# Attention's transpositions and 64-wide scores on halves of the array's rows, in common sections, with all eight PSUM banks in one ring

## The chip, the core and the metric

The kernel runs on one core of one Trainium2 chip. A core has a matrix engine (TensorE, with an array of 128 rows and 128 columns), VectorE, ScalarE, GpSimd, a queue that issues transfers (SyncE), an on-chip memory of 128 partitions (SBUF), and eight accumulation banks (PSUM) into which TensorE writes. The metric is the device time of one execution in microseconds; lower is better. In the profile PE is TensorE's matmuls, PEld its weight loads, DVE VectorE, ACT ScalarE, POOL GpSimd and SP SyncE.

## What is computed

A trunk of two layers over 512 tokens of width 1024, all in float32. Each layer has three attentions side by side on one projection of the normed input, a gated sum of them, and a feed-forward part with a short convolution. The parts that matter here are the three attentions:

```python
z_na, c_q, c_kv, k_rope, z_gq, z_gkv, z_gate = jnp.split(h @ w_in, offs, axis=-1)
# A, neighbourhood: 8 heads of 64, grid of 8 x 64 tokens, 16 columns around each, bias by position
s = jnp.einsum('bqhd,brqchd->bhqrc', q_r, k_win) * scale + bias
p = jax.nn.softmax(s.reshape(B, H, GRID_W, win_r * NA_WIN_C), axis=-1)
out = jnp.einsum('bhqrc,brqchd->bqhd', p, v_win)
# B, latent: 4 heads, 128 plain values and 64 rotary ones, the rotary key shared by the heads
s = (jnp.einsum('bqhd,bkhd->bhqk', qn, k_nope) + jnp.einsum('bqhr,bkr->bhqk', qp, k_pe)) * scale
o = jnp.einsum('bhqk,bkhd->bqhd', jax.nn.softmax(s, axis=-1), v)
# C, window: 8 heads of 64 on 2 key heads, blocks of 128 with their neighbours, a sink logit per head
s = jnp.einsum('bnqkgd,bnjkd->bnkgqj', qb, kw) * scale
p = jax.nn.softmax(jnp.concatenate([s, sink_b], axis=-1), axis=-1)[..., :-1]
o = jnp.einsum('bnkgqj,bnjkd->bnqkgd', p, vw)
merged = gates[0] * (y_na @ w_br_na) + gates[1] * (y_mla @ w_br_mla) + gates[2] * (y_gqa @ w_br_gqa)
```

## The kernel before

Everything is kept transposed: channels lie on partitions, the 512 tokens along the free dimension. TensorE's operands are of the type fp32r. To keep float32's accuracy each operand is a pair of a high part (rounded to fp32r, by ScalarE) and a low part (the rest, by VectorE); `split` (L147) makes the pair. A product is then three matmuls, high x high, high x low and low x high (`mm3`, L159, its matmuls on L164 to L166). `dense` (L168) is such a product over a weight block that `fetch` (L109) loads from memory and splits ahead of time; a block over 1024 channels is 24 matmuls of 128x128 weights and 512 moving columns.

The order of the work is a list of steps written by hand in `schedule` (L251, the list from L290); `run` calls `do_<step>` for each, and TensorE and the transfer queue keep that order. ScalarE and VectorE are ordered by a scheduler, in which the attention's steps (`ATTN`, L38) have priority. Dense steps (`gate`, `br`, `qn`, `kn`, `naq`, `gq` and so on) stand between the attention's steps.

Each attention has the same stages. Scores are formed by TensorE in a bank (`do_ms` L515 latent, `do_ns` L634 neighbourhood, `do_gs` L781 window). VectorE and ScalarE make the softmax of them in a tile `pt`. TensorE turns 128x128 blocks of `pt` by a transposing matmul, in which the block is loaded as weights and an identity (`idf`) streams through (`do_mt` L536, `do_nt` L666, `do_gt` L823, on L540, L671 and L830). `split` takes the turned blocks out of the bank into a pair `ph`, `pl`, and TensorE multiplies that with the values (`do_mp`, `do_np`, `do_gp`).

Where a score runs over 64 values only, half of the array's rows would be empty. The kernel before fills them: `stack` (L225) puts the high part of a query (or key) on 64 partitions and its low part on the other 64, `swap` (L230) makes a copy with the halves exchanged, and two matmuls over all 128 rows give all four products of high and low parts. They are L523 and L524 (the rotary part of the latent scores, 512 columns), L652 and L653 (neighbourhood, 256 columns), L799 and L800 (window, 384 columns, or 256 at the ends).

The banks are given out by `bank` (L103) from groups that each stage sets with `banks`: in the latent attention two for dense products, three for scores, two for turned blocks and one for the values' product. A step takes the next bank of its group, and waits until that was read. The steps are fine-grained: a latent head's scores come as two halves of two query blocks, its sixteen blocks are turned in two halves of eight, and each half is followed by half of the values' product.

Of the kernel before, what the change touches and what calls it, by code (L numbers as in the profile page):

```python
# [17 lines left out]
P = 128  # L18
L = 2
D = 1024  # L20
S = 512
# [16 lines left out]
ATTN, ATTN_PRIO = ("ms", "mt", "mp", "ns", "nt", "np", "gs", "gt", "gp"), 100  # L38
RAWB, WB, GZB, GPB, PRIO = 3, 3, 5, 3, 300
HALVES = ((slice(0, 64), slice(64, 128)), (slice(64, 128), slice(0, 64)))  # L40
# [18 lines left out]
class Trunk:  # L59
# [153 lines left out]
    def rope(self, pool, ps, rows, ct, st, nb=2):  # L213
        nc = self.nc
        sw = pool.tile([P, S], F32, tag="ph", name="rsw", bufs=nb)
# [3 lines left out]
        t = pool.tile([P, S], F32, tag="pl", name="rot", bufs=nb)  # L219
        self.mul(t[:rows], ps[:rows], ct[:rows])  # L220
        self.mul(sw[:rows], sw[:rows], st[:rows])
        nc.vector.tensor_add(t[:rows], t[:rows], sw[:rows])
        return t

    def stack(self, dst, src, half):  # L225
        a, b = HALVES[half]
        self.nc.scalar.copy(dst[a], src[a])
        self.nc.vector.tensor_sub(dst[b], src[a], r32(dst)[a])

    def swap(self, dst, src):  # L230
        self.nc.scalar.copy(dst[0:64], r32(src)[64:128])
        self.nc.scalar.copy(dst[64:128], r32(src)[0:64])
# [18 lines left out]
    def schedule(self, l):  # L251
# [39 lines left out]
        s += [("kn", 0), gate(), "mla_attn", ("qn", 1), ("kn", 1), ("ms", 0, 0), ("ms", 0, 1), gate()]  # L291
# [4 lines left out]
        s += [gate(), ("mt", 3, 0), ("nak", 0), ("mp", 3, 0), ("mt", 3, 1), ("nav", 0), ("mp", 3, 1)]  # L296
        s += ["na_open", ("nvt", 0), ("ns", 0), ("naq", 1), ("ns", 1), ("nav", 1), ("br", 1, 0), ("nt", 0)]
        s += [("nak", 1), ("np", 0), ("nt", 1), ("br", 1, 1), gate(), ("np", 1)]
        for p in (1, 2):
            h = 2 * p  # L300
            s += [("nvt", p), ("ns", h), ("naq", p + 1), ("ns", h + 1), ("nav", p + 1), ("nt", h)]
            s += [("nak", p + 1), ("np", h), ("nt", h + 1), ("br", 1, p + 1), gate(), ("np", h + 1)]
        s += [("nvt", 3), ("ns", 6), ("br", 1, 4), ("ns", 7), ("br", 1, 5), gate(), ("nt", 6)]
        s += [("br", 1, 6), gate(), ("np", 6), ("nt", 7), ("br", 1, 7), gate(), ("np", 7)]
        s += ["gq_open", "gk", ("gq", 0), "gv", ("gq", 1), "gvt", gate(), ("br", 0, 0), ("br", 0, 1)]
        s += [("gs", 0, 0), ("gq", 2), ("gs", 0, 1), ("gq", 3)]
# [3 lines left out]
        s += [("gt", 7, 0), ("gt", 7, 1), gate(), ("gp", 7), "br012", ("br", 2, 3)]  # L310
# [144 lines left out]
    def do_kr(self):  # L455
# [11 lines left out]
        self.stack(self.kr[0], t, 0)  # L467
        self.swap(self.kr[1], self.kr[0])
# [19 lines left out]
    def do_qr(self):  # L488
        st = self.weights(self.spec())
        self.qr = []  # L490
        for i in range(2):
# [3 lines left out]
            for j in range(2):  # L495
                q = self.mp.tile([P, S], F32R, tag=f"qr{2 * i + j}", name="qr")
                self.stack(q, t, j)
                self.qr.append(q)

    def do_mla_attn(self):  # L500
        self.banks(d=[0, 1], s=[2, 3, 4], tp=[5, 6], po=[7])
# [13 lines left out]
    def do_ms(self, h, half):  # L515
        nc, mm = self.nc, self.nc.tensor.matmul
        for b in (2 * half, 2 * half + 1):
            bs = slice(b * P, (b + 1) * P)
            s = self.bank("s")
            mm(s, self.qn[h][0][:, bs], self.kn[h][0], start=True, stop=False)  # L520
            mm(s, self.qn[h][0][:, bs], self.kn[h][1], start=False, stop=False)
            mm(s, self.qn[h][1][:, bs], self.kn[h][0], start=False, stop=False)
            mm(s, self.qr[h][:, bs], self.kr[0], start=False, stop=False)  # L523
            mm(s, self.qr[h][:, bs], self.kr[1], start=False, stop=True)  # L524
            nm = self.small.tile([P, 2], F32, tag="nm", name="nm", bufs=6)
            pt = self.mp2.tile([P, S], F32, tag="pt", name="pt", bufs=6)
# [9 lines left out]
    def do_mt(self, h, half):  # L536
        for kc in (2 * half, 2 * half + 1):
            tp = self.bank("tp")
            for b in range(4):
                self.nc.tensor.transpose(tp[:, b * P:(b + 1) * P], self.pts[h, b][:, kc * P:(kc + 1) * P], self.idf)  # L540
            self.pp[h, kc] = [self.mp2.tile([P, S], F32R, tag=t, name=t, bufs=2) for t in ("ph", "pl")]
            self.split(*self.pp[h, kc], tp)

    def do_mp(self, h, half):
        if half == 0:
            self.po = self.bank("po")
        kcs = (2 * half, 2 * half + 1)
        hs = slice(h * P, (h + 1) * P)
        self.mm3(self.po, [tuple(v[:, hs] for v in self.V[kc]) for kc in kcs], [self.pp[h, kc] for kc in kcs],
                 half == 0, half == 1)  # L550
        if half == 1:
            self.y[1, h] = self.ypair("ya", h)
            self.split(*self.y[1, h], self.po)

    def do_na_open(self):
        nc = self.nc  # L560
        self.banks(d=[0, 1, 2], s=[3, 4], tp=[5, 6], po=[7])
# [18 lines left out]
    def do_naq(self, p):  # L580
        ps = self.dense(self.spec(), self.h)
        if p == 0:
            self.q1, self.q2, self.k1, self.vt, self.vs, self.nc_ = {}, {}, {}, {}, {}, {}
# [6 lines left out]
    def na_q(self, p):  # L590
        for j in range(2):
            h = 2 * p + j
            self.q1[h] = self.np.tile([P, S], F32R, tag="q1", name="q1", bufs=3)
            self.q2[h] = self.np.tile([P, S], F32R, tag="q2", name="q2", bufs=3)
            self.stack(self.q1[h], self.nc_["q", p], j)
            self.swap(self.q2[h], self.q1[h])
# [9 lines left out]
    def na_k(self, p):  # L606
        for j in range(2):
            k = self.np.tile([P, S + P], F32R, tag="k1", name="k1", bufs=3)
            self.pad(r32(k))
            self.stack(k[:, 64:576], self.nc_["k", p], j)  # L610
            self.k1[2 * p + j] = k
# [22 lines left out]
    def do_ns(self, h):  # L634
        nc, mm = self.nc, self.nc.tensor.matmul
        tm = self.np.tile([P, 3, 256], F32, tag="tm", name="tm")
        nc.vector.tensor_tensor(tm, self.nmask, self.tb[h][:].rearrange("p (o k) -> p o k", o=1).to_broadcast([P, 3, 256]), ALU.add)
        if h + 4 < 8:
            self.na_table(h + 4)
# [467 lines left out]
```

## Time and profile before

| | |
|---|---|
| median of 3 runs | 1702.47 us (1701.95 to 1702.61) |
| profiled execution, from its first to its last instruction | 1700.3 us |
| the median stands above that span by | 2.2 us |
| granted TensorE clock | 1.000 |
| instructions of the profiled execution | 21121 |
| transfers | 155.38 MB, mean 91 GB/s |

A group line of the profile reads: line, engine, operation, what it writes and reads, partitions and elements, count, then busy time and mean duration in ns, then the engine's idle time before it. A matmul's duration is longer than its distance to the next one, since matmuls are pipelined; busy time counts overlapping ones once. Only the times given in ns or us here come from the trace; the order listings below have none.

### The profile page before, as it was taken

What the parts mean: (1) busy time and instruction counts of PE and PEld (TensorE: products, weight loads), DVE (VectorE), ACT (ScalarE), POOL (GpSimd) and SP (SyncE); (2) the same over time, 40 slices, a digit from 0 to 9 for tenths busy, and PEclk for the clock granted to TensorE, in tenths of its full rate; (3) what the DMA queues carried; (4) which work ended last, traced back from release to release, by engine and by line L of the source; (5) the groups of instructions that cost most, each with busy time, mean ns of one, the idle gap of its engine ahead of it and who ended that gap; (6) DMA issues with size and microseconds to landing.
All of it is one profiled execution on the core that took longest, in us unless ns stands there. A gap on an engine that the chain in (4) does not pass through costs nothing.

```text
span 1700.3 us, 21121 instructions
## 1 busy us (share of the span) xinstructions
PE 1693.9 (100%) x7922; PEld 1415.7 (83%) x7922; DVE 1144.9 (67%) x1873; ACT 867.3 (51%) x1505; POOL 53.4 (3%) x107
## 2 busy tenths in 40 slices
PE   9999999999999999999999999999999999999998
PEld 8888888888888888888888888888888888888887
DVE  7767885887558777734367678768766587777234
ACT  7665555775435444433256656557744444444232
POOL 1100000000000000000011100000000000000000
PEclk9999999999999999999999999999999999999999
DMA  5323233222323333323233232332223333333231
GB/s 178 84 79 84 82 93 87 75 69 75 106 85 115 98 100 99 99 87 100 81 96 81 82 85 67 109 84 69 63 81 107 98 112 99 94 93 98 87 105 69
DMA packets 289399, 155.38 MB, mean 91 GB/s; under 512 B 8881, under 2 KB 285377, under 8 KB 289297
## 3 DMA queue, kind: packets, MB, share of 16 engines
q1 hardware_dynamic: 286752, 148.88, 30.6%
q0 software_dynamic: 2256, 4.83, 0.9%
q8 instruction: 62, 1.02, 0.3%
q14 instruction: 41, 0.33, 0.1%
q10 hardware_dynamic: 288, 0.33, 0.1%
HBM read 151.89 MB, written 2.10 MB: 91 GB/s over the span
## 4 chain that ended last, share of the span: by engine, by line
PE 96%; DVE 0%; DMA 0%; issue 0%; ACT 0%; ACTq 0%
PE ps_d L166 21%; PE ps_d L164 21%; PE ps_d L165 21%; PE ps_g L166 7%; PE ps_g L165 7%; PE ps_g L164 7%; PE ps_tp L830 1%; PE ps_po L686 1%; PE ps_tp L540 1%; PE ps_tp L671 1%; PE ps_s L800 1%; PE ps_s L799 1%; PE ps_po L845 1%; PE ps_po L844 1%; PE ps_s L653 0%; PE ps_s L652 0%
## 5 line engine op out<-in xcount | busy, mean ns | idle before, releaser
L150 ACT CAST whi<-raw 128x1024 fp32r<-128x1024 f32 (+4 forms) x339 | 301.3, 889 | 573.5 <-PE ps_d L165 344.4
L164 PE MATMUL ps_d<-hh,whi 128*128 128x512 f32 x1285 | 501.0, 390 | 0.0
L166 PE MATMUL ps_d<-hh,wlo 128*128 128x512 f32 x1285 | 500.3, 389 | 0.0
L165 PE MATMUL ps_d<-hl,whi 128*128 128x512 f32 x1285 | 500.2, 389 | 0.0
L151 DVE TENSOR_TENSOR wlo<-raw,whi 128x1024 fp32r<-128x1024 f32 (+4 forms) x337 | 344.6, 1023 | 174.3 <-ACT whi L150 173.5
L166 PEld LDWEIGHTS ps_d<-hh,wlo 128*128 128x128 f32 x1285 | 241.2, 188 | 50.5 <-DVE wlo L151 0.2
L165 PEld LDWEIGHTS ps_d<-hl,whi 128*128 128x128 f32 x1285 | 241.3, 188 | 49.6
L164 PEld LDWEIGHTS ps_d<-hh,whi 128*128 128x128 f32 x1285 | 241.3, 188 | 49.6 <-DVE rot L157 0.3
L164 PE MATMUL ps_g<-ff,whi 128*128 128x512 f32 x334 | 129.9, 389 | 0.0
L165 PE MATMUL ps_g<-ff,whi 128*128 128x512 f32 x334 | 129.9, 389 | 0.0
L166 PE MATMUL ps_g<-ff,wlo 128*128 128x512 f32 x334 | 129.9, 389 | 0.0
L157 DVE TENSOR_TENSOR u<-ps_d,rb 128x512 f32<-128x512 f32 x80 | 55.3, 691 | 63.1 <-PE ps_d L166 63.1
L157 DVE TENSOR_TENSOR gz<-ps_d,rb 128x512 f32<-128x512 f32 x48 | 33.1, 690 | 82.1 <-PE ps_d L166 82.0
L164 PEld LDWEIGHTS ps_g<-ff,whi 128*128 128x128 f32 x334 | 62.7, 188 | 13.1
L165 PEld LDWEIGHTS ps_g<-ff,whi 128*128 128x128 f32 x334 | 62.7, 188 | 13.1
L166 PEld LDWEIGHTS ps_g<-ff,wlo 128*128 128x128 f32 x334 | 62.7, 188 | 12.8
L151 DVE TENSOR_TENSOR pl<-ps_tp,ph 128x512 fp32r<-128x512 f32 x104 | 68.5, 684 | 3.1 <-ACT ph L150 2.9
L900 ACT ACTIVATE c<-c 128x512 f32<-128x512 f32 x44 | 27.8, 631 | 80.5 <-DVE c L896 80.4
L150 ACT CAST ph<-ps_tp 128x512 fp32r<-128x512 f32 x104 | 56.8, 585 | 3.6 <-PE ps_tp L540 2.8
L157 DVE TENSOR_TENSOR c<-c 128x512 f32<-128x512 f32 x44 | 30.5, 693 | 31.4 <-ACT c L900 31.4
L164 PE MATMUL ps_d<-yah,whi 128*128 128x512 f32 x128 | 50.8, 397 | 0.0
L166 PE MATMUL ps_d<-yah,wlo 128*128 128x512 f32 x128 | 49.9, 390 | 0.0
(315 smaller groups left out, 2728.1 us busy)
## 6 DMA issues: line engine op xcount, KB each, us to landing
raw<-in_w_in_dram SPq DMA_DIRECT2D x86, 512.0 KB, 4.0
raw<-in_w_up_dram SPq DMA_DIRECT2D x80, 512.0 KB, 3.9
raw<-in_w_down_dram SPq DMA_DIRECT2D x32, 512.0 KB, 4.2
raw<-in_w_down_dram SPq DMA_DIRECT2D x16, 384.0 KB, 3.5
raw<-in_w_in_dram SPq DMA_DIRECT2D x17, 256.0 KB, 2.9
raw<-in_w_br_mla_dram SPq DMA_DIRECT2D x16, 256.0 KB, 2.7
raw<-in_w_br_na_dram SPq DMA_DIRECT2D x16, 256.0 KB, 2.7
raw<-in_w_br_gqa_dram SPq DMA_DIRECT2D x16, 256.0 KB, 2.8
```

Of the source, the lines that this page charges most:

```text
L150: nc.scalar.copy(hi, src)
L151: nc.vector.tensor_sub(lo, src, r32(hi))
L157: self.nc.vector.tensor_tensor(out, a, b, ALU.mult)
L164: mm(ps, sh, mh, start=first and k == 0, stop=False)
L165: mm(ps, sh, ml, start=False, stop=False)
L166: mm(ps, sl, mh, start=False, stop=last and k == n - 1)
L540: self.nc.tensor.transpose(tp[:, b * P:(b + 1) * P], self.pts[h, b][:, kc * P:(kc + 1) * P], self.idf)
L671: self.nc.tensor.transpose(tp[:, i * P:(i + 1) * P], self.pts["n", h, bp][:, i // 2, (i % 2) * P:(i % 2) * P + P], self.idf)
L686: nc.tensor.matmul(pq[:, qs], self.vs[p][:, ch, j, :], pm[:].rearrange("p (k c) -> p k c", c=P)[:, ks], start=i == 0 and m == 0, stop=i == ...
L799: mm(s, q, self.gk[g][0][:, ks], start=not (pair and j), stop=False)
L800: mm(s, q, self.gk[g][1][:, ks], start=False, stop=not pair or j == 1)
L900: nc.scalar.activation(c, c, AF.Gelu_apprx_tanh)
```

## The change

The array is used as two halves of 64 rows where an operand has only 64 values, and for the attention's transpositions.

`rowed` multiplies with pairs of half-height matmuls: for each of the three products of high and low parts, one on partitions 0 to 63 and one on 64 to 127, with their own weights, moving data and bank. Queries and keys are therefore no longer stacked: `split` makes their pairs as they are, two heads lying one above the other. In the latent attention one head has 64 rotary values, so the halves take different query blocks of the same head: for every other block a copy with the halves exchanged is made (`qo`), and the rotary key lies in both halves (`both`). `turned` transposes a block as two half-height transpositions of 64 columns each, into two banks; `unfold` takes them out again with one `split` per bank, writing runs of 64 columns.

The step list is rewritten so that half-height steps stand next to each other: a head's (or pair's, or block's) transpositions are directly followed by the next one's half-height scores. The latent scores are cut in two for that, `mr` (the rotary part, half-height) and `ms` (the plain part, whole, and the softmax). Steps are coarser: all sixteen blocks of a head are turned in one step, both heads of a neighbourhood pair are scored in one step, and all four heads of a window block too. Dense steps move accordingly. From `mla_attn` on, the eight banks form one ring from which every step takes the next.

Some pools change their tags and numbers of buffers, and the scratch space for software-made transfers is set to 2048.

```diff
+ROWS = (slice(0, 64), slice(64, 128))
+HALVES = (ROWS, ROWS[::-1])
...
     def bank(self, g):
+        if g not in self.groups:
+            g = "ring"
         b = self.groups[g][self.turn[g] % len(self.groups[g])]
...
-    def stack(self, dst, src, half):
-        a, b = HALVES[half]
-        self.nc.scalar.copy(dst[a], src[a])
-        self.nc.vector.tensor_sub(dst[b], src[a], r32(dst)[a])
-
-    def swap(self, dst, src):
-        self.nc.scalar.copy(dst[0:64], r32(src)[64:128])
-        self.nc.scalar.copy(dst[64:128], r32(src)[0:64])
+    def turned(self, blocks):
+        out = [self.bank("tp") for _ in range(2)]
+        for n, block in enumerate(blocks):
+            for i, q in enumerate(ROWS):
+                self.nc.tensor.transpose(out[i][:, n * 64:n * 64 + 64], block[q], self.idf[q, q])
+        return out
+
+    def unfold(self, hi, lo, turned, n):
+        for i in range(2):
+            self.split(*(t.rearrange("p (n i c) -> p i n c", i=2, c=64)[:, i] for t in (hi, lo)),
+                       turned[i][:, :n * 64].rearrange("p (n c) -> p n c", c=64))
+
+    def rowed(self, outs, sts, mvs, first=True, last=True):
+        for t, (a, b) in enumerate(((0, 0), (0, 1), (1, 0))):
+            for out, st, mv in zip(outs, sts, mvs):
+                self.nc.tensor.matmul(out, st[a], mv[b], start=first and t == 0, stop=last and t == 2)
+
+    def both(self, hi, lo, src, rows):
+        nc = self.nc
+        a, b = HALVES[rows]
+        nc.scalar.copy(hi[a], src[a])
+        nc.scalar.copy(hi[b], src[a])
+        nc.vector.tensor_sub(lo[a], src[a], r32(hi)[a])
+        nc.scalar.copy(lo[b], r32(lo)[a])
...
         for h in range(3):
-            dn = [("qn", h + 2), ("kn", h + 2)] if h < 2 else [("naq", 0)]
-            s += [("ms", h + 1, 0), ("mt", h, 0)] + dn + [("mp", h, 0), ("mt", h, 1), ("ms", h + 1, 1)]
-            s += ([gate()] if h == 1 else []) + [("mp", h, 1)]
...
+            s += [("mt", h), ("mr", h + 1), ("ms", h + 1)]
+            s += [("qn", h + 2), ("kn", h + 2)] if h < 2 else [("naq", 0)]
+            s += [("mp", h)] + ([gate()] if h == 1 else [])
...
+        s += [("nav", 2), ("np", 2), ("np", 3), ("nvt", 2), ("naq", 3), ("nak", 3), ("br", 1, 2), gate(), ("nt", 2), ("ns", 3)]
...
         for i in range(7):
-            s += [("gt", i, 0), ("gt", i, 1), ("gs", i + 1, 0), ("br", 0, i + 1) if i else gate(), ("gp", i)]
-            s += [("gs", i + 1, 1), gate()]
...
+            s += [("gt", i), ("gs", i + 1), ("br", 0, i + 1) if i else gate(), ("gp", i), gate()]
...
     def do_mla_attn(self):
-        self.banks(d=[0, 1], s=[2, 3, 4], tp=[5, 6], po=[7])
+        self.banks(ring=list(range(8)))
...
+    def do_mr(self, h):
+        self.sb = [self.bank("s") for _ in range(4)]
+        own, other = self.qr[h // 2]
+        for u in range(2):
+            sts = []
+            for r, q in enumerate(ROWS):
+                c = (2 * u + r) * P
+                sts.append([w[q, c:c + P] if r == h % 2 else o[q, u * P:u * P + P] for w, o in zip(own, other)])
+            self.rowed(self.sb[2 * u:2 * u + 2], sts, [[k[q, :] for k in self.kr] for q in ROWS], last=False)
...
+                self.rowed([banks[bp][j][:, e * 256:e * 256 + 256] for j in range(2)],
+                           [[t[q, b * P:(b + 1) * P] for t in self.q[p]] for q in ROWS],
+                           [[t[q, b * P:b * P + 256] for t in self.k[p]] for q in ROWS])
...
+            self.rowed(sp[-2:], [[t[q, b * P:(b + 1) * P] for t in self.gqs[2 * g + half]] for q in ROWS],
+                       [[t[q, ks] for t in self.gk[g]] for q in ROWS])
```

Two places show how TensorE's rows move. The first is the latent attention, where one head's transpositions meet the next head's scores. Before: `kn,qn` and `kr,qr` are the plain and the rotary part of one query block's scores, `ps_tp` a bank of turned blocks, and `ps_d<-mg` the next dense product.

```order
L520 MATMUL ps_s<-kn,qn 128x512
L521 MATMUL ps_s<-kn,qn 128x512
L522 MATMUL ps_s<-kn,qn 128x512
L523 MATMUL ps_s<-kr,qr 128x512
L524 MATMUL ps_s<-kr,qr 128x512
L540 MATMUL ps_tp<-idf,pt 128x128 x8
L164 MATMUL ps_d<-mg_286,whi 128x512
```

Now, at the same place, `qo` is the exchanged copy of the query, and every bank is called `ps_ring`:

```order
L169 MATMUL ps_ring<-ph,ynl_656 128x512
L234 MATMUL ps_ring<-idf,pt 128x64 x32
L247 MATMUL ps_ring<-kr,qr 128x512
L247 MATMUL ps_ring<-kr,qo 128x512
...
L167 MATMUL ps_ring<-kn,qn 128x512
L168 MATMUL ps_ring<-kn,qn 128x512
L169 MATMUL ps_ring<-kn,qn 128x512
L167 MATMUL ps_ring<-kn,qn 128x512
```

Eight whole transpositions and two rotary matmuls in each block's scores became thirty-two half transpositions and twelve half-height matmuls (two are shown) in one stretch, with the values' product ahead of it and the plain part of the scores behind.

The second is the window attention, at a query block with three key blocks. Before, with `gk,gq` the scores of two heads:

```order
L830 MATMUL ps_tp<-idf,pt 128x128 x12
L799 MATMUL ps_s<-gk,gq 128x384
L800 MATMUL ps_s<-gk,gq 128x384
L799 MATMUL ps_s<-gk,gq 128x384
L800 MATMUL ps_s<-gk,gq 128x384
L164 MATMUL ps_d<-ynh_1798,whi 128x512
```

Now, with the scores of four heads in twelve half-height matmuls:

```order
L169 MATMUL ps_ring<-hh,wlo 128x512
L234 MATMUL ps_ring<-idf,pt 128x64 x24
L247 MATMUL ps_ring<-gk,gq 128x384 x12
L167 MATMUL ps_ring<-ynh_1925,whi 128x512
L168 MATMUL ps_ring<-ynl_1926,whi 128x512
```

The other two heads' scores, which stood behind the values' product, moved up to the first two, next to the transpositions; a dense branch product follows as before.

More of the change, by code (lines that the diff above doesn't have):

```diff
@@ L311, in schedule @@
+        s += [("gt", 7), gate(), ("gp", 7), "br012", ("br", 2, 3)]
         for m in range(4, 7):
@@ L534, in do_ms, with do_mt, do_mp @@
             self.pts[h, b] = pt
[L536 to L547, printed above, removed]
-        hs = slice(h * P, (h + 1) * P)
[L549 to L553, printed above, removed]
+    def do_mt(self, h):
+        turned = [self.turned([self.pts[h, b][:, kc * P:(kc + 1) * P] for kc in kcs for b in range(4)])
+                  for kcs in ((0, 1), (2, 3))]
+        for u in range(2):
+            pair = [self.mp2.tile([P, 2 * S], F32R, tag=t, name=t, bufs=2) for t in ("ph", "pl")]
+            self.unfold(*pair, turned[u], 8)
+            for e in range(2):
+                self.pp[h, 2 * u + e] = [t[:, e * S:(e + 1) * S] for t in pair]
+    def do_mp(self, h):
+        po = self.bank("po")
+        hs = slice(h * P, (h + 1) * P)
+        self.mm3(po, [tuple(v[:, hs] for v in self.V[kc]) for kc in range(4)], [self.pp[h, kc] for kc in range(4)])
+        self.y[1, h] = self.ypair("ya", h)
+        self.split(*self.y[1, h], po)
     def do_na_open(self):
         nc = self.nc
-        self.banks(d=[0, 1, 2], s=[3, 4], tp=[5, 6], po=[7])
         self.mps.close()
@@ L590, in na_q @@
     def na_q(self, p):
[L591 to L596, printed above, removed]
+        self.q[p] = [self.np.tile([P, S], F32R, tag=f"q{n}", name="nq") for n in "hl"]
+        self.split(*self.q[p], self.nc_["q", p])
     def do_nak(self, p):
@@ L632, in do_nvt, with do_ns @@
         self.yf = self.const.tile([P, S], F32, tag="acc", name="yf")
[L634 to L639, printed above, removed]
-        elif h == 4 and self.l == 0:
-            gmf = self.np.tile([P, 2 * P], F32, tag="tb", name="gmf", bufs=4)
-            nc.gpsimd.dma_start(gmf, self.d["gmask"])
-            nc.vector.memset(self.gmask, 0.0)
-            gm = self.gmask[:].rearrange("p (k c) -> p k c", c=P)
-            nc.vector.tensor_copy(gm[:, 0::2], gmf[:].rearrange("p (k c) -> p k c", c=P))
+    def do_ns(self, p):
+        nc = self.nc
+        banks = [[self.bank("s") for _ in range(2)] for _ in range(2)]
@@ L676, in do_np, with do_nt @@
+    def do_nt(self, p):
+        for h in (2 * p, 2 * p + 1):
+            turned = self.turned([self.pts["n", h, bp][:, e, k * P:(k + 1) * P]
+                                  for bp in range(2) for e in range(2) for k in range(2)])
+            self.pp["n", h] = [self.np2.tile([P, 2 * S], F32R, tag=t, name=t, bufs=2) for t in ("ph", "pl")]
+            self.unfold(*self.pp["n", h], turned, 8)
     def do_np(self, h):
@@ L774, in do_gq @@
     def do_gq(self, i):
[L775 to L784 removed]
+        t = self.rope(self.gp, self.dense(self.spec(), self.h), P, self.rc, self.rsn, ("rsw", "rot"), 2)
@@ L790, in do_gs @@
-        nm = self.gnm
-        hs = 2 * half
         m0 = P if b == 0 else 0
-        pair = nk == 2
-        bank = self.bank("s") if pair else None
-        sp = []
-        for j in range(2):
-            s = bank[:, j * w:(j + 1) * w] if pair else self.bank("s")[:, :w]
-            q = self.gqs[4 * g + hs + j][:, bs]
-            mm(s, q, self.gk[g][0][:, ks], start=not (pair and j), stop=False)
-            mm(s, q, self.gk[g][1][:, ks], start=False, stop=not pair or j == 1)
-            sp.append(s)
@@ L818, in do_gs @@
[L818 to L833 removed]
+        nm = self.small.tile([P, 12], F32, tag="gnm", name="nm", bufs=3)
@@ new lines, in do_gt @@
+    def do_gt(self, i):
+        nk = self.span(i)[3]
+        blocks = [self.pts["g", i, hh][:, kb * P:(kb + 1) * P] for kb in range(nk) for hh in range(4)]
+        parts = [blocks[n:n + 8] for n in range(0, len(blocks), 8)]
+        turned = [self.turned(part) for part in parts]
+        pair = [self.gp.tile([P, 3 * S], F32R, tag=t, name=t) for t in ("ph", "pl")]
+        for u, part in enumerate(parts):
+            n = len(part)
+            self.unfold(*(t[:, u * 1024:u * 1024 + n * P] for t in pair), turned[u], n)
+        for kb in range(nk):
+            self.pp["g", i, kb] = [t[:, kb * S:(kb + 1) * S] for t in pair]
```

212 lines of the change are left out of this document (97 added, 115 removed).

## The prediction

> **What bounds the kernel now.** I read the busy times first, then the chain that ended last, then who waited for whom on TensorE.
>
> ```profile
> PE 1693.9 (100%) x7922; PEld 1415.7 (83%) x7922; DVE 1144.9 (67%) x1873; ACT 867.3 (51%) x1505; POOL 53.4 (3%) x107
> ...
> PE 96%; DVE 0%; DMA 0%; issue 0%; ACT 0%; ACTq 0%
> ...
> PE idle L343 <- DVE cst L84: 1.0, 1, 1.0
> PE ps_s L520 <- DVE pt L527: 0.2, 1, 0.2
> ```
>
> TensorE works all the time: 1693.9 of 1700.3 us, 96% of the chain, and in the whole program the table of waits finds 1.2 us in which it stood for somebody. So this kernel's time is a sum over TensorE's instructions, each counted at the distance to the next one's start (a matmul's own duration includes a tail that lies beside its successor). Work that another engine saves or adds is worth nothing unless TensorE comes to wait for it.
>
> These are the groups by form that the change touches, both layers together: first the transpositions, then the second term of the latent attention's scores, then the scores of the neighbourhood and of the window attention.
>
> ```profile
> L830 PE MATMUL ps_tp<-idf,pt 128*128 128x128 f32 x160 | 20.6, 274 | 0.0
> L540 PE MATMUL ps_tp<-idf,pt 128*128 128x128 f32 x128 | 16.6, 272 | 0.0
> L671 PE MATMUL ps_tp<-idf,pt 128*128 128x128 f32 x128 | 16.6, 272 | 0.0
> L523 PE MATMUL ps_s<-kr,qr 128*128 128x512 f32 x32 | 12.5, 392 | 0.0
> L524 PE MATMUL ps_s<-kr,qr 128*128 128x512 f32 x32 | 12.5, 390 | 0.0
> L652 PE MATMUL ps_s<-k,q 128*128 128x256 f32 x64 | 16.6, 292 | 0.0
> L653 PE MATMUL ps_s<-k,q 128*128 128x256 f32 x64 | 16.0, 283 | 0.0
> L799 PE MATMUL ps_s<-gk,gq 128*128 128x384 f32 x32 | 11.4, 357 | 0.0
> L800 PE MATMUL ps_s<-gk,gq 128*128 128x384 f32 x32 | 10.8, 337 | 0.0
> L799 PE MATMUL ps_s<-gk,gq 128*128 128x256 f32 x32 | 8.7, 295 | 0.0
> L800 PE MATMUL ps_s<-gk,gq 128*128 128x256 f32 x32 | 8.3, 280 | 0.0
> ```
>
> Their counts are 160 + 128 + 128 = 416 transpositions, 64 matmuls over 512 columns, 64 over 384, and 128 + 64 = 192 over 256. Their distances come from the timeline of TensorE, at one place for each width (start, duration, line):
>
> ```profile
> 77.27 0.39 PE L523 MATMUL ps_s<-kr,qr 128*128 128x512 f32 x1
> 77.50 0.39 PE L524 MATMUL ps_s<-kr,qr 128*128 128x512 f32 x1
> 77.73 1.03 PE L540 MATMUL ps_tp<-idf,pt 128*128 128x128 f32 x8
> 78.52 0.48 PE L164 MATMUL ps_d<-mg,whi 128*128 128x512 f32 x1
> 78.83 0.40 PE L165 MATMUL ps_d<-mg,whi 128*128 128x512 f32 x1
> ...
> 142.28 0.28 PE L652 MATMUL ps_s<-k,q 128*128 128x256 f32 x1
> 142.40 0.28 PE L653 MATMUL ps_s<-k,q 128*128 128x256 f32 x1
> ...
> 315.65 0.33 PE L800 MATMUL ps_s<-gk,gq 128*128 128x384 f32 x1
> 315.82 0.34 PE L799 MATMUL ps_s<-gk,gq 128*128 128x384 f32 x1
> 316.00 0.34 PE L800 MATMUL ps_s<-gk,gq 128*128 128x384 f32 x1
> ```
>
> 512 columns take 0.23 us (77.27, 77.50, 77.73; 0.227 over longer runs), 384 take 0.175, 256 take 0.12. The eight transpositions: the L165 matmul at 78.83 is one distance behind the true start of L164, which is therefore 78.60; (78.60 - 77.73) / 8 = 0.109 each. What is touched now costs 416 x 0.109 = 45.3, 64 x 0.227 = 14.5, 64 x 0.175 = 11.2 and 192 x 0.12 = 23.0: 94 us of 1700.
>
> **Is a transposition bound by its weight load or by its columns?** Everything hangs on this, because halving leaves every load with 128 columns, and doubles their number. One place tells: the engine stood still for data just before 314.87, and the loads (PEld) start again one by one.
>
> ```profile
> 314.87 0.14 PEld L830 LDWEIGHTS ps_tp<-idf,pt 128*128 128x128 f32 x1
> ...
> 314.93 0.14 PEld L830 LDWEIGHTS ps_tp<-idf,pt 128*128 128x128 f32 x1
> ...
> 315.04 0.14 PEld L830 LDWEIGHTS ps_tp<-idf,pt 128*128 128x128 f32 x1
> ...
> L830 PEld LDWEIGHTS ps_tp<-idf,pt 128*128 128x128 f32 x160 | 18.4, 140 | 2.6 <-DVE pt L817 0.3
> L653 PEld LDWEIGHTS ps_s<-k,q 128*128 128x128 f32 x64 | 12.2, 191 | 0.3
> ```
>
> With no matmul in flight the second load follows the first by 0.06 us; with one in flight the third follows by 0.11. So a transposition's load takes at most 0.06, and the 0.109 is its 128 columns (twice the 0.42 ns a column that 256 against 512 columns give: (0.227 - 0.12) / 256). A score's load lasts 191 against 140 ns, about 0.05 longer: 0.06 + 0.05 = 0.11, and under the 0.12 at which matmuls with a load each follow one another.
>
> **The change part by part.**
>
> *Transpositions.* 416 become 416 pairs: two instructions over 64 columns, one on rows 0 to 63, one on rows 64 to 127, into two banks. No row here shows two row halves at once, so the pair is bounded from both sides: if the halves run side by side, half of the columns, 0.056 (which is also the load's 0.06); if they take turns, 0.112. I take 0.056, because nothing in the rows is shared by the two: other rows of the array, other partitions read, another bank written. 416 x (0.109 - 0.056) = 22.0 us less.
>
> *Scores.* Two full-height matmuls (stacked high and low parts) become three half-height ones per head, in pairs: three pairs where four matmuls were, of the same width. Side by side: 16 x 0.227 + 32 x 0.12 + 16 x 0.175 + 16 x 0.12 = 3.6 + 3.8 + 2.8 + 1.9 = 12.1 us less. In turns: 32 x 0.227 + 32 x 0.175 + 96 x 0.12 = 24.4 us more.
>
> *Switches.* The order of the changed program has 38 sections of half-height work (five in the latent, five in the neighbourhood and nine in the window attention, twice), so 76 changes between whole and halved array. None is in the trace. The lower bound is nothing. The upper bound is an array that must run empty and load anew:
>
> ```profile
> L166 PE MATMUL ps_d<-hh,wlo 128*128 128x512 f32 x1285 | 500.3, 389 | 0.0
> ```
>
> 389 ns long at a distance of 227, so 0.16 us are in flight behind each start; with a load of 0.11 exposed, 0.27. I take the middle, 0.135: 76 x 0.135 = 10.3 us more (0 to 20.5). The Trainium skill says that this is a real cost: "TensorEngine Tiling (Array Packing)", Key Properties, has it that a change of tiling mode, not of tile alone, drains the engine. It gives no figure; by that rule the zero end falls away and the sum moves toward the other end.
>
> *Covers.* The order is coarser. In the latent attention a head's sixteen blocks are turned at once, after all four softmax rows of that head; their cover is qn, kn and the values' product, 9 + 6 + 12 matmuls x 0.227 = 6.1 us. A late softmax would hold the transpositions and, behind them in TensorE's queue, the next head's scores and everything dense. The window attention's cover is 12 + 6 + 24 matmuls, 9.5 us, where the second half of a block had only the gate's 5.4. What the other engines do in these stretches (columns: stretch, its length, then busy time of PE, PEld, DVE, ACT, POOL):
>
> ```profile
> 75.40:141.30 65.90, 65.90 (x323) 54.89 (x322) 46.23 (x89) 40.35 (x74) 4.49 (x12) 1.00 0.29 81
> 175.00:205.60 30.60, 30.60 (x163) 26.25 (x162) 26.36 (x47) 18.92 (x39) 1.63 (x6) 1.00 0.31 87
> 302.40:399.40 97.00, 97.00 (x486) 82.22 (x485) 78.40 (x196) 72.68 (x180) 0.00 (x0) 1.00 0.25 70
> ```
>
> VectorE is busy 70, 86 and 81%. TensorE's time in them would shrink by 3 to 6%, so nobody overtakes it. I set 2 us for late softmaxes and banks (0 to 6; less than nothing is excluded, since only 1.2 us of waiting is there to be won).
>
> *The rest, at nothing, all behind TensorE.* Splitting query and key whole instead of stacking halves saves copies: 18 on ScalarE and 10 subtractions on VectorE per layer, counted in the code, the window attention's extra splits included. The turned banks are unfolded into runs of 64 columns with gaps; such a write exists already, and costs what a plain one does:
>
> ```profile
> L150 ACT CAST vs<-ps_tp x10: 587/587/588, 142.1 to 1136.0; 128x512 fp32r<-128x512 f32 x10
> L151 DVE TENSOR_TENSOR vs<-ps_tp,vs x10: 679/681/684, 143.2 to 1137.2; 128x512 fp32r<-128x512 f32 x10
> ...
> L150 ACT CAST ph<-ps_tp 128x512 fp32r<-128x512 f32 x104 | 56.8, 585 | 3.6 <-PE ps_tp L540 2.8
> L151 DVE TENSOR_TENSOR pl<-ps_tp,ph 128x512 fp32r<-128x512 f32 x104 | 68.5, 684 | 3.1 <-ACT ph L150 2.9
> ```
>
> Bias tables, masks and weights are fetched in the order of the steps; SP's queue and POOL (3% busy) pass no new wait. If that cover went, a late table would cost what the first reader waits, some us once.
>
> *Sum.* -22.0 - 12.1 + 10.3 + 2 = -21.8 us. Against the profiled execution: 1700.3 to 1678.5. The median of the runs shown is 2.2 us above that span, so 1702.5 - 21.8 = **1680.7 us**. With both unknown costs at their low ends 1668.4; at their high ends -34.1 + 20.5 + 6 = -7.6, 1694.9.
>
> **The rivals.**
>
> *Loads of the two halves take turns* (slower than before). In the trace no two loads run side by side, though nothing there has disjoint rows. Then a score pair costs at least 2 x 0.11 = 0.22 whatever its width: nothing changes at 512 columns (-3.6), 48 x 0.22 - 11.2 = -0.6 at 384, but (96 + 48) x 0.22 - 23.0 = +8.7 at 256; transposition pairs cost 0.112, +1.2. Sum +5.7, with switches and covers +18.0: 1720 (1708 to 1735). It decides from where a 256-column pair passes 0.16 and a transposition pair 0.109.
>
> *The halves don't overlap at all*, so that the change does not do what it says: +1.2 + 24.4 + 12.3 = +37.9, 1740. Against it: separate rows and separate banks, alternating in the order.
>
> *Transpositions get no faster.* If a load of 64 rows kept 0.109 to itself, only the scores would gain: -12.1 + 12.3, 1702.7 (1690 to 1715). The rows at 314.87 speak against it, with 0.06. The Trainium skill speaks for it: "TensorE: Matmul & The Clock Gate", LDWEIGHTS (loading the stationary operand), states that a load takes its columns divided by 1.2 per ns, whatever its rows. By that rule 128 columns take 107 ns; the trace does not agree for these loads, and the measurement decides.
>
> *Covers too short.* If each of the 38 sections waited 0.5 us for softmax or a bank, +19 would stand in place of the 2: 1697.7. Against it, the shares above.
>
> **How the numbers follow.** Forecast 0.68; transpositions no faster 0.09; covers 0.05; loads in turns 0.12; no overlap 0.06. The range from 1668 to 1712 holds the forecast's own 1668 to 1695, the covers, nearly all of the third rival and the foot of the first: 0.83. About 0.2%, 3.4 us, is what a measurement here can tell from no change. Faster by more: 0.68 + 0.03 (covers) + 0.03 (third rival) = 0.74. Within: 0.02 + 0.03 = 0.05. Slower by more: 0.03 + 0.12 + 0.06 = 0.21.
>
> **What would show it.** In the changed profile: half-height matmuls of a pair starting nearly together; 32 half transpositions in 0.9 us; twelve half-height matmuls over 512 columns in 1.4 us; a gap of 0.1 to 0.2 us at each change of height; the table of waits for TensorE still near 1 us. Wrong if 32 half transpositions take 1.7 us or more, if 256-column pairs come at 0.2 us, or if TensorE waits for VectorE or ScalarE by tens of us.

## The result and the profile after

| | |
|---|---|
| the changed kernel, median | 1705.62 us (1702.83 to 1707.39, 19 runs) |
| the kernel before, run beside it | 1701.99 us (1701.24 to 1704.05, 19 runs) |
| ratio | 1.0018 (95% interval 1.0011 to 1.0025) |
| profiled execution, from its first to its last instruction | 1705.3 us (before 1700.3) |
| granted TensorE clock | 0.997 (before 1.000) |

The change costs 3.6 us, where 21.8 us of gain were forecast. The profile's page and the table of waits of TensorE, in the changed kernel, stand here in the places of those that opened the prediction (a wait's numbers are its total in us, how often, and the longest):

```profile
PE 1684.6 (99%) x8498; PEld 1388.1 (81%) x8498; DVE 1119.1 (66%) x1853; ACT 830.5 (49%) x1469; POOL 52.4 (3%) x107
...
PE 94%; DVE 5%; ACT 1%; issue 0%; ACTq 0%
```

```profile
PE ps_ring L642 <- DVE nm L680: 7.4, 4, 1.9
PE ps_ring L167 <- DVE pl L154: 4.0, 10, 0.7
PE ps_ring L642 <- DVE vt L160: 1.5, 2, 0.8
PE idle L361 <- DVE cst L85: 1.0, 1, 1.0
PE ps_ring L855 <- DVE pl L154: 0.7, 2, 0.4
PE ps_ring L247 <- DVE gq L154: 0.6, 2, 0.3
```

TensorE is busy 9 us less than before (1684.6 against 1693.9) and yet ends 5 us later: it now waits 15.2 us, nearly all for VectorE, where it waited 1.2. VectorE's own share has not grown (66%, before 67%), so the waits come from when its work is done, not from how much there is.

What the change set out to do, it does. This is TensorE's timeline in the changed kernel, from the last dense matmul ahead of a head's transpositions to the plain part of the next head's scores:

```profile
74.26 0.39 PE L169 MATMUL ps_ring<-hh,wlo 128*128 128x512 f32 x1
74.58 1.22 PE L234 MATMUL ps_ring<-idf,pt 64*128 64x64 f32 x32
75.60 0.48 PE L247 MATMUL ps_ring<-kr,qo 64*128 64x512 f32 x1
75.61 0.47 PE L247 MATMUL ps_ring<-kr,qr 64*128 64x512 f32 x1
75.93 0.39 PE L247 MATMUL ps_ring<-kr,qr 64*128 64x512 f32 x1
...
76.86 0.39 PE L247 MATMUL ps_ring<-kr,qr 64*128 64x512 f32 x1
77.18 0.50 PE L167 MATMUL ps_ring<-kn,qn 128*128 128x512 f32 x1
77.52 0.39 PE L168 MATMUL ps_ring<-kn,qn 128*128 128x512 f32 x1
```

Two halves start 0.01 us apart, and a pair of 512 columns has the distance of one whole matmul: from 75.93 to 76.86, four pairs, 0.23 each. The 32 half transpositions take 75.60 - 74.58 = 1.02 us, 0.064 a pair where a whole one took 0.109. Behind them the first pair of scores takes 0.32 us to the next (75.61 to 75.93), a seam inside the section. The changes of height are in the same rows: 0.32 instead of 0.227 from 74.26 to 74.58, 0.32 from 76.86 to 77.18, and 0.34 from 77.18 to 77.52. Over all 38 sections, the start distances at and right behind the changes come to 0.36 us a section above their usual, 13.6 us in all.

The lost time is elsewhere. In the neighbourhood attention the values' transposition (the step `nvt`, L642) stands right behind the products `np` of the pair before (L702). TensorE and VectorE in the changed kernel at the first such place:

```profile
169.39 0.28 PE L702 MATMUL ps_ring<-pl,vs 128*128 128x256 f32 x1
171.53 0.63 PE L642 MATMUL ps_ring<-idf,vt 128*128 128x128 f32 x4 [1.86 <-DVE nm L680]
...
172.73 0.63 PE L167 MATMUL ps_ring<-hh,whi 128*128 128x512 f32 x1
173.16 0.63 PE L168 MATMUL ps_ring<-hl,whi 128*128 128x512 f32 x1
```

```profile
161.28 1.88 DVE L154 TENSOR_TENSOR pl<-ps_ring,ph 128x512 fp32r<-128x512 f32 x3
...
164.88 1.28 DVE L674 SCALAR_TENSOR_TENSOR pt<-ps_ring,tm 128x512 f32<-128x512 f32 x2
166.07 1.86 DVE L677 TENSOR_REDUCE nm<-pt 128x2 f32<-128x512 f32 x3
167.85 0.95 DVE L661 TENSOR_TENSOR tm<-nmask,tb 128x768 f32<-128x768 f32 x1
...
169.31 0.95 DVE L661 TENSOR_TENSOR tm<-nmask,tb 128x768 f32<-128x768 f32 x1
170.18 0.22 DVE L680 RECIPROCAL nm<-nm 128x2 f32<-128x2 f32 x2
170.31 1.07 DVE L160 TENSOR_TENSOR vt<-ps_ring,rb 128x448 f32<-128x448 f32 x2
```

VectorE has no pause from 161.28 to the scaled values `vt` at 170.31 (the rows left out lie in between without a gap): it unfolds the turned blocks of both heads, adds the bias to both heads' scores, reduces them, and makes two bias sums `tm` (0.95 us each) for the next pair. TensorE stands from 169.39 to 171.53, 2.14 us from start to start where 0.12 is usual. The table names `nm`, which stands just ahead of `vt` in VectorE's order; what TensorE's transposition reads is `vt`. Before, both sides had room (VectorE, then TensorE):

```profile
155.06 1.13 DVE L157 TENSOR_TENSOR vt<-ps_d,rb 128x448 f32<-128x448 f32 x2
```

```profile
174.67 0.60 PE L628 MATMUL ps_tp<-idf,vt 128*128 128x128 f32 x4
```

The values lay ready from about 156.2 for 18.5 us. The second thing that TensorE's rows of the changed kernel show, at 172.73, is matmuls 0.43 us apart, not 0.23. The same kernel's stretch there and the one behind it (start and end, length, busy PE, PEld, DVE, ACT, POOL, then the granted clock, in which 1.00 is full):

```profile
172.70:176.10 3.40, 3.40 (x9) 2.63 (x8) 3.34 (x10) 1.09 (x2) 0.00 (x0) 0.51 0.58 154
176.10:180.00 3.90, 3.90 (x18) 3.19 (x17) 1.64 (x4) 0.88 (x1) 0.00 (x0) 1.00 0.02 4
```

After the wait TensorE runs at half its clock for 3.4 us, and loses half of that, some 1.6 us (eight matmuls 0.43 apart instead of 0.23). There are three such stretches in this execution, behind three of the four waits of some 2.14 us.

### The profile page after: what moved, and what is told of

The parts are those of the page before. It is cut to its first block, busy times and chain, and to the rows that moved or that the text cites. A ratio compares the mean times of both kernels' runs of the same rounds, so it can differ in the third digit from the quotient of the medians.

```text
span 1705.3 us, 22226 instructions
## 1 busy us (share of the span) xinstructions
PE 1684.6 (99%) x8498; PEld 1388.1 (81%) x8498; DVE 1119.1 (66%) x1853; ACT 830.5 (49%) x1469; POOL 52.4 (3%) x107
## 4 chain that ended last, share of the span: by engine, by line
PE 94%; DVE 5%; ACT 1%; issue 0%; ACTq 0%
PE ps_ring L167 12%; PE ps_ring L168 12%; PE ps_ring L169 12%; PE ps_d L168 11%; PE ps_d L169 11%; PE ps_d L167 10%; PE ps_g L167 7%; PE ps_g L169 7%; PE ps_g L168 7%; PE ps_ring L247 1%; DVE pl L154 1%; PE ps_ring L234 1%; DVE pt L674 1%; DVE nm L677 1%; PE ps_g L267 1%; PE ps_ring L855 1%
## 5 line engine op out<-in xcount | busy, mean ns | idle before, releaser
L169 PE MATMUL ps_d<-hh,wlo 128*128 128x512 f32 x685 | 266.6, 389 | 0.0
L168 PE MATMUL ps_d<-hl,whi 128*128 128x512 f32 x685 | 266.5, 389 | 0.0
L167 PE MATMUL ps_d<-hh,whi 128*128 128x512 f32 x685 | 266.5, 389 | 0.0
L167 PE MATMUL ps_ring<-hh,whi 128*128 128x512 f32 x600 | 236.7, 395 | 0.5 <-DVE pl L154 0.5
L168 PE MATMUL ps_ring<-hl,whi 128*128 128x512 f32 x600 | 235.4, 392 | 0.0
L169 PE MATMUL ps_ring<-hh,wlo 128*128 128x512 f32 x600 | 235.2, 392 | 0.0
L167 PEld LDWEIGHTS ps_d<-hh,whi 128*128 128x128 f32 x685 | 128.6, 188 | 26.9
L167 PEld LDWEIGHTS ps_ring<-hh,whi 128*128 128x128 f32 x600 | 113.8, 190 | 25.3 <-DVE pl L154 1.2
L169 PEld LDWEIGHTS ps_ring<-hh,wlo 128*128 128x128 f32 x600 | 113.7, 190 | 24.3
L168 PEld LDWEIGHTS ps_ring<-hl,whi 128*128 128x128 f32 x600 | 113.7, 190 | 23.7
L167 PE MATMUL ps_g<-ff,whi 128*128 128x512 f32 x334 | 129.9, 389 | 0.0
L167 PEld LDWEIGHTS ps_g<-ff,whi 128*128 128x128 f32 x334 | 62.7, 188 | 13.0
```

Source lines behind the costliest of these rows:

```text
L167: mm(ps, sh, mh, start=first and k == 0, stop=False)
L168: mm(ps, sh, ml, start=False, stop=False)
L169: mm(ps, sl, mh, start=False, stop=last and k == n - 1)
```

## The experiments

The theory: the halves and the sections work as forecast, and what is lost is the cover of TensorE's own order, above all at `nvt`, plus the half clock that these waits call up. The rivals: VectorE binds in these stretches, so that a wait which is removed comes back further on; or the halves themselves are worth less than their distances say.

**The values' transposition later.** The steps are only put in another order:

```diff
-("np", 1), ("nvt", 1), ("naq", 2), ("nak", 2), ("br", 1, 1), ...
+("np", 1), ("naq", 2), ("nvt", 1), ("nak", 2), ("br", 1, 1), ...
-("np", 3), ("nvt", 2), ("naq", 3), ("nak", 3), ...
+("np", 3), ("naq", 3), ("nvt", 2), ("nak", 3), ...
-("np", 5), ("nvt", 3), ("br", 1, 3), gate(), ("br", 1, 4), ...
+("np", 5), ("br", 1, 3), gate(), ("nvt", 3), ("br", 1, 4), ...
```

> The changed kernel with the three later transpositions of the values (nvt 1, 2 and 3) moved behind the next dense step. Theory (a step of the order came too close to what it reads: the six waits of 2.0, 2.0 and 0.9 us ahead of L642 per layer, and the three stretches of 3.4 us at half clock behind them): 9.9 + 5.1 us less, 1690.6 us, clock 1.000. Rival (VectorE has too much to do in this stretch, so the wait comes back at the next step): less than 3 us gained, 1703 or more.

Measured: 1692.85 us (1692.26 to 1693.33), ratio to before 0.9942 (0.9930 to 0.9955), span 1691.4. TensorE's waits in this version:

```profile
PE ps_ring L167 <- DVE pl L154: 4.0, 10, 0.7
...
PE ps_ring L855 <- DVE pl L154: 0.7, 2, 0.4
```

Both rows of L642 are gone, the other rows are as they were, and nothing of size came in their place. One step, moved at three places of the list, took 13.9 us out of the span (12.8 between the medians); the start distances at L642 had been 9.97 above their usual (4 x 2.02 and 2 x 0.95), and the three stretches at half clock some 4.8. That VectorE binds in these stretches is refuted.

**VectorE's order by priority.** The first attempt on VectorE's side gave the step that makes `vt` the attention's priority:

```diff
-ATTN, ATTN_PRIO = ("mr", "ms", ...
+ATTN, ATTN_PRIO = ("nav", "mr", "ms", ...
```

> The changed kernel's order on TensorE untouched, but the step that writes the values' tile (nav) gets the attention's priority on VectorE and ScalarE. Theory (the tile's product stood late in VectorE's queue, behind softmax and bias additions that nobody needed yet): the waits ahead of L642 fall below 0.5 us and the time to about 1691 us. Rival (VectorE's sum of work binds): another step waits instead, 1702 or more.

Measured: 1706.01 us (1703.88 to 1709.61), ratio 1.0022 (1.0013 to 1.0032), span 1703.4. This was a miss: the priority left `vt` at its place behind the reductions, and the waits stayed:

```profile
PE ps_ring L642 <- DVE nm L680: 7.4, 4, 1.9
...
PE ps_ring L642 <- DVE vt L160: 1.6, 2, 0.8
```

It tells one thing by the way: with the same four waits of 2.10 to 2.14 us its profiled execution has one stretch at half clock, not three. How often the clock falls behind such a wait differs from execution to execution. That fits the wide spread of the two kernels that have these waits (4.6 and 5.7 us, against 1.1 of the version without them). Each run has its own mean granted clock, and the time goes with it: one stretch of 3.4 us at half clock is 0.001 of the mean, and of the changed kernel's 19 runs the fastest (1702.83 us) has 1.000, the two slowest (1707.08 and 1707.39) 0.997. By these runs some 2.8 of the 3.6 us that the change cost (1705.62 - 1702.83) go with the clock; without it the change is no gain either, since even that fastest run is not below the median of the kernel before (1701.99).

**Two additions less on VectorE.** TensorE's order stays the changed kernel's; the bias sums `tm` go to GpSimd:

```diff
-            nc.vector.tensor_tensor(tm, self.nmask, ...
+            nc.gpsimd.tensor_tensor(tm, self.nmask, ...
```

> The changed kernel with TensorE's order untouched and only the sums of mask and bias (the two additions of 0.95 us each that stand between the reductions and the values' scaling in VectorE's queue) given to GpSimd. Theory (the values' transposition waits for its values because VectorE works without a pause ahead of them; the long waits of 1.9 us then call up stretches at half the TensorE clock): the values come some 1.3 us sooner (1.9 us less, one product of 0.35 us and one reciprocal of 0.15 us now ahead of them), the four waits of 1.86 us fall to some 0.6 us each, -5, and with them the stretches at half clock may go, -4 to -5: 1696, 1694 to 1701. Rival (the wait stands for something else, as ScalarE's share of the values' path or TensorE's own order, or it moves to the next step): no change, 1705.6; or GpSimd's additions come too late and delay the scores, above 1706.

Measured: 1700.80 us (1700.15 to 1702.86), ratio 0.9990 (0.9981 to 0.9999), span 1698.7, 6.6 less than the changed kernel's. VectorE and TensorE at the same place as above:

```profile
168.84 1.07 DVE L682 TENSOR_SCALAR pt<-pt,nm 128x256 f32<-128x256 f32 x2
...
169.91 1.07 DVE L160 TENSOR_TENSOR vt<-ps_ring,rb 128x448 f32<-128x448 f32 x2
```

```profile
169.61 0.28 PE L702 MATMUL ps_ring<-pl,vs 128*128 128x256 f32 x1
171.13 0.63 PE L642 MATMUL ps_ring<-idf,vt 128*128 128x128 f32 x4 [1.24 <-DVE vt L160]
...
171.82 0.39 PE L168 MATMUL ps_ring<-h,whi 128*128 128x512 f32 x1
172.05 0.39 PE L169 MATMUL ps_ring<-h,wlo 128*128 128x512 f32 x1
```

The wait shrinks with VectorE's queue, so VectorE's order is its cause from this side too. It shrinks by half of what was expected, to 1.24 us (start to start 1.52): with the additions gone, two products of the softmax (L682, 1.07 us together) slipped in ahead of `vt`. And behind 1.52 us no matmul runs at half clock: this execution has no such stretch at all, which is more than half of its gain by the 4.8 us above.

**The short part first.** In the window attention the twelve blocks of a query block with three key blocks are turned as eight and then four. The dense step behind the scores takes the ninth bank of the ring, counted from the first turned one, which is that same bank, and waits until it is unfolded: 0.73 us at each of four places, most of the row of L167 above (the other six waits in it are 0.18 each). The first of the four, in the changed kernel:

```profile
330.58 1.30 PE L247 MATMUL ps_ring<-gk,gq 64*128 64x384 f32 x12
332.62 0.50 PE L167 MATMUL ps_ring<-ynh,whi 128*128 128x512 f32 x1 [0.73 <-DVE pl L154]
```

This version is the one with `nvt` late, and turns the four first:

```diff
-        parts = [blocks[n:n + 8] for n in range(0, len(blocks), 8)]
+        n0 = len(blocks) % 8 or 8
+        parts = [blocks[:n0]] + [blocks[n:n + 8] for n in range(n0, len(blocks), 8)]
```

> The first experiment, and in the window attention the part of four blocks is turned before the part of eight, so that the first bank of the ring is emptied sooner. Theory (the dense product behind a section takes the ring's ninth bank, which is the first turned one, and waits 0.84 us for its unfolding, four times, and 0.1 to 0.4 elsewhere): 2 to 3 us less than the first experiment, about 1688. Rival (the unfolding is late because VectorE is, not because of its order): within 1 us of the first.

Measured: **1689.84 us** (1689.38 to 1690.95), ratio 0.9926 (0.9914 to 0.9939), span 1689.1: 3.0 below the version before it, and the fastest of all. The four waits of 0.73 us are gone. What is left of TensorE's waits for unfolding:

```profile
PE ps_ring L858 <- DVE pl L154: 1.4, 4, 0.4
PE ps_ring L167 <- DVE pl L154: 1.1, 6, 0.2
```

**Another cover in the window attention.** To cover what is left, the gate's dense step goes ahead of the values' product:

```diff
-("br", 0, i + 1) if i else gate(), ("gp", i), gate()]
+("br", 0, i + 1) if i else gate(), gate(), ("gp", i)]
```

> The version with the values' transposition late and the short part of the window attention's transposition first, and with the gate's dense step put ahead of the product of probabilities and values instead of behind it. Theory (what is left of the lost time is TensorE waiting for the unfolding of transposed blocks on VectorE and ScalarE, and a dense step of 3 to 4 us between them covers it): the waits for pl, 2.5 us in the version before it, fall under 0.5 us, 1687 to 1688. Rival (the wait only moves to the dense step's own bank, or the products' banks are released later): within 0.7 us of that version, 1689.8, or above it.

Measured: 1711.59 us (1711.38 to 1712.47), ratio 1.0053 (1.0040 to 1.0065), 21.8 above the version before it. The theory of this step failed. Its rival had the cause in words (the products' banks are released later), but no size for it: "within 0.7 us of that version, 1689.8, or above it". The new row in the table of waits, and TensorE at one of the four places:

```profile
PE ps_ring L247 <- DVE yf L865: 13.9, 4, 3.5
```

```profile
324.75 0.95 PE L247 MATMUL ps_ring<-gk,gq 64*128 64x384 f32 x7
329.18 1.30 PE L247 MATMUL ps_ring<-gk,gq 64*128 64x384 f32 x5 [3.48 <-DVE yf L865]
...
331.00 0.63 PE L168 MATMUL ps_ring<-ynl,whi 128*128 128x512 f32 x1
331.43 0.63 PE L169 MATMUL ps_ring<-ynh,wlo 128*128 128x512 f32 x1
```

The waits for the unfolding at L858 did go. But the gate had been standing behind the product, and was the cover of something else. Counted in the ring from the product's bank, four turned banks and four for the scores follow; the eighth, which is the product's own again, falls to the eighth of the twelve half-height scores, and just there TensorE stops, after seven, until VectorE has read the product out (`yf`, L865). With the gate between, VectorE had 24 matmuls' time more. Behind each of these waits matmuls stand at 0.43 us too (here from 331.00 to 331.43). The waits make 13.9 of the 21.8 us. Most of the rest can be estimated from the granted clock: some 19 us of work ran at half of it, which loses 9.5 us, and the 1.4 of waits at L858 went.

**Whole transpositions.** The version with `nvt` late, with each block turned whole again, and the turned blocks taken out of their banks as they lie; scores, sections and banks stay:

```diff
-            for i, q in enumerate(ROWS):
-                self.nc.tensor.transpose(out[i][:, n * 64:n * 64 + 64], block[q], self.idf[q, q])
+            self.nc.tensor.transpose(out[n // 4][:, n % 4 * P:n % 4 * P + P], block, self.idf)
```

> The first experiment, with whole transpositions of 128 columns in place of the pairs of halves. Theory (halves run side by side, 0.066 against 0.109 us a block, and a change of height costs 0.15): 416 x 0.043 = 17.9 us more, less 12 changes x 0.15 = 1.8: 16 us above the first experiment, about 1707. Rival (the halves bring little, since each section pays for them): within 4 us of the first.

Measured: 1703.08 us (1702.36 to 1704.52), ratio 1.0002 (0.9993 to 1.0011), 10.2 above the version with halves. So the halves do pay, and the rival falls. They pay less than expected mostly because with them a part comes back as waits (4.7 us at L167 and L855 in the table of the version with `nvt` late); with the slower transpositions the unfolding keeps up, and TensorE waits for nothing but this:

```profile
PE idle L359 <- DVE cst L85: 1.0, 1, 1.0
PE ps_ring L245 <- DVE gq L154: 0.6, 2, 0.3
```

**Halves in the old order.** The kernel before takes over the half transpositions alone, in the latent and the neighbourhood attention, each at its old place (some buffers are regrouped to hold the wider pairs):

```diff
-            for b in range(4):
-                self.nc.tensor.transpose(tp[:, b * P:(b + 1) * P], self.pts[h, b][:, kc * P:(kc + 1) * P], self.idf)
...
+        self.halved(banks, [self.pts[h, b][:, kc * P:(kc + 1) * P] for kc in (2 * half, 2 * half + 1) for b in range(4)])
```

> The kernel before with one thing taken over: the transpositions of the first attention's and the neighbourhood attention's probabilities by halves, at the places where the whole ones stood. That is 256 blocks in 32 sections; scores, order of work and banks stay as they were before. Theory (a pair of half transpositions costs 0.065 us instead of 0.109, and a section costs 0.36 us for its two changes of height): 256 x -0.044 = -11.3 and 32 x 0.36 = +11.5, so no change within 2 us of the kernel before, 1702. That would show that the changes of height, which the changed kernel puts into common sections, eat the whole gain if each step has a section of its own. Rival (changes of height cost nothing themselves, what stood beside them in the changed kernel were waits): 11 us faster, 1691.

Measured: 1701.37 us (1700.73 to 1702.06), ratio 0.9993 (0.9984 to 1.0001); the span is 1699.8, 0.5 below before's. One of its 32 sections:

```profile
77.58 0.39 PE L534 MATMUL ps_s<-kr,qr 128*128 128x512 f32 x1
77.90 0.72 PE L228 MATMUL ps_tp<-idf,pt 64*128 64x64 f32 x16
78.54 0.50 PE L164 MATMUL ps_d<-mg,whi 128*128 128x512 f32 x1
78.88 0.39 PE L165 MATMUL ps_d<-mg,whi 128*128 128x512 f32 x1
```

Eight pairs should take 8 x 0.064 = 0.51. From 77.58 to 78.88 stand 1.30 us; two whole matmuls and the pairs make 0.227 x 2 + 0.51 = 0.97, so the two changes of height cost 0.33, and the pairs save 8 x 0.045 = 0.36. A section of eight blocks just about pays for itself. This kernel waits for nobody there, so the price of the switch is one of its own, and common sections are what makes halves worth anything. The Trainium skill, "TensorEngine Tiling (Array Packing)", Key Properties, says that a change of mode drains the engine, without a figure. These rows agree that a change has a price, and give it a figure; that the engine runs empty in between they do not show, since the first half-height row starts at 77.90, before the recorded end of the whole matmul ahead of it (77.58 + 0.39 = 77.97).

**The halves in turns.** The version with `nvt` late writes each six half-height scores as three of the upper half, then three of the lower:

```diff
-        for t, (a, b) in enumerate(((0, 0), (0, 1), (1, 0))):
-            for out, st, mv in zip(outs, sts, mvs):
+        for out, st, mv in zip(outs, sts, mvs):
+            for t, (a, b) in enumerate(((0, 0), (0, 1), (1, 0))):
```

> The version with the values' transposition moved later, in which each group of six half-height score matmuls is written in turns by threes (all three of the upper half of the rows, then all three of the lower) instead of alternating half by half. The scores are 48 pairs of 512 columns, 48 of 384 and 144 of 256, at 0.227, 0.175 and 0.12 us a pair: 36.6 us in all. Theory (a matmul overlaps only the instruction next to it in TensorE's order, as the alternation of the changed kernel supposes): of six matmuls in a row only the two on each seam between the halves run side by side, so four to six slots stand where three stood: 12 us (a third of 36.6) to 37 us longer, 1705 to 1730. Rival (the two halves have queues of their own that run ahead of each other, so the order within a group doesn't matter): within 2 us of the alternating version, 1692.9.

Measured: 1693.12 us (1693.01 to 1693.21), ratio 0.9944 (0.9928 to 0.9959), 0.3 above the alternating version. TensorE's timeline; in the program three matmuls with `qr` stand ahead of three with `qo`:

```profile
65.34 0.49 PE L247 MATMUL ps_ring<-kr,qr 64*128 64x512 f32 x1
65.35 0.49 PE L247 MATMUL ps_ring<-kr,qo 64*128 64x512 f32 x1
```

My theory fell. The first `qo` starts 0.01 us behind the first `qr`, with two more `qr` ahead of it in the program: at least three instructions deep, each half runs its own, and the order between the halves does not matter. The same page of the Trainium skill, Key Properties, says that tiles operate independently; this run agrees.

## Why the prediction was wrong

*Transpositions, -22.0.* Right in mechanism, a little too large: a pair takes 0.064, not 0.056, so 416 x (0.109 - 0.064) = 18.7 less. The rival by which they get no faster fell.

*Scores, -12.1.* Right: pairs have the distance of one whole matmul of their width. Both rivals on halves that take turns or don't overlap fell. (That in the trace of before no two loads run side by side was misread: of the two loads at 314.87 and 314.93 each is recorded with 0.14 us, so they overlap.)

*Switches, +10.3.* Right in that a change costs, and inside the bounds (0 to 20.5): 13.6 measured, 0.18 instead of 0.135 a change. The 0.135 was the middle between two bounds, so its closeness is partly luck.

*Covers, +2 (0 to 6).* **This is the step that failed.** The start distances of the changed kernel give 9.97 at `nvt`, 3.4 at the dense step behind the window attention's scores (four times 0.84), 2.4 at smaller waits for a bank or an operand, and three half-clock stretches of 1.6: 20.6 us in place of 2. The sum is then -18.7 - 12.1 + 13.6 + 20.6 = +3.4. The span grew by 5.0 and the median by 3.6. The 1.6 us by which the span exceeds the sum are about the seam inside the sections, for which neither the forecast nor a rival had a term: the first pair of scores behind the transpositions takes 0.32 us to the next instead of 0.23, and itself comes 0.03 sooner than one more pair of transpositions would, so 0.06 a section and 1.5 us over the 26 sections that have both.

The reasoning behind the 2 us went wrong in three ways. It looked for covers where softmax rows are turned, named those (6.1 and 9.5 us), and found them sufficient, and so they are: no wait for a softmax appears. But the same rewritten list had moved `nvt` from 18.5 us behind its values to 1.9 us of other work (sixteen matmuls of 0.12), and that step was not among those costed. It read VectorE's share over 31 to 97 us (70 to 86%) as proof that nobody overtakes TensorE, when a queue in order can be busy for 10 us on end within such a share: here from 160 to 170, because both heads' scores now come at once. And it did not count the ring's banks through, by which the dense step meets the first turned bank. "If TensorE waits for VectorE or ScalarE by tens of us" stood in the text as what would make it wrong, and 15 us, with the clock's 5 behind them, come near to that. The halved clock behind a wait of 2 us stood nowhere in the forecast.

The rival "covers too short" had the right kind of mechanism, but spread it evenly over 38 sections, and gave it 0.05. That its +19 us lie so near to the 20.6 is luck: half of these stand at six places with a step that it did not name, and another 4.8 are the clock's. It is luck too that 1705.6 lies between 1668 and 1712: the upper part of that range was kept for transpositions that get no faster and for loads in turns, and neither came. (The third rival's upper end of 1715 is 1717 by its own terms, 1702.5 - 12.1 + 20.5 + 6; nothing hangs on it.) With the covers mended, the forecast's sign holds: 1689.84 us, 12.8 below the run of before beside it (1702.61). What still separates that from the forecast's 21.8 are the switches and the transpositions (3.3 each), the seams (1.5) and the covers (about 2 more than the 2 allowed); these estimates add up to 10, where 9.0 are missing between the medians and 10.6 between the spans.

## What to carry to other kernels

When a step list is made coarser, go through every step that moved, those too that the change is not about, and ask for each operand when the engine that makes it will come to it in its own queue, counting what now arrives there at once; an engine's share over tens of us does not answer that. In a ring of banks, count through whose bank each step is given. Work on half of the array pays per section and not per instruction: on this shape a section had to hold more than eight transposed blocks before it gained anything clear of the noise.

## What the runs showed of the hardware

- A wait of some 2 us can halve TensorE's clock for one stretch of 3.4 us. Behind waits of 2.10 to 2.14 us from start to start (1.82 to 1.86 idle) it did so three times of four in one execution and once of four in another; behind some 1.5 us never in the execution with four of them; and behind the waits of the version with the gate moved (3.48 us idle, 3.8 from start to start) at all four places, for 3.4 us at one and 6.8 at three of them. The Trainium skill, "TensorE: Matmul & The Clock Gate", Part 1, gives the window as 3.4 us and free-running, which fits the length, and also that the three stretches of one execution begin whole multiples of 3.413 us apart (at 172.63, 1015.72 and 1049.86 us: 247 and 10 times). Its rule of thumb (HAM oscillation), that gaps over about 3.4 us do the harm, does not fit, since here 1.86 us of idle were enough. Why one wait brings a stretch and an equal one does not, these runs do not show.
- The halves of the array are fed independently, three instructions deep at least: a `qo` matmul with two `qr` ahead of it in the program started 0.01 us behind the first `qr`.
- The two changes of a section, into halves and back, cost 0.33 to 0.36 us together: 0.09 on the way in, 0.09 + 0.11 on the way back, and most of the rest at the first pair of half transpositions, which stands 0.11 us ahead of the next where later pairs stand 0.06 apart.
